# Half of an output projection as seven block products instead of eight, with operand sums and the residual formed by loads that add

## The chip, the core and the metric

The kernel runs on one core of a Trainium2 chip. The core has a matrix engine (TensorE, "PE" in the profile; its weight loads are "PEld"), a vector engine (VectorE, "DVE"), a scalar engine (ScalarE, "ACT"), GpSimd ("POOL") and SyncE ("SP"). All of them can issue DMA transfers, and 16 DMA engines carry these out between the chip's memory (HBM) and the on-chip memory SBUF. TensorE writes into PSUM banks, from which DVE or ACT must fetch the results ("evacuate" them). A load may also add what it reads to what stands in SBUF; in this kernel all such adding loads are issued by POOL. The metric is the device time of one execution in microseconds (us).

## What is computed

One transformer-like block over 512 tokens (rows) of width 2048, all in float32. Cut to what matters here:

```python
h = rmsnorm(x, norm_mix_pre)
proj = h @ w_in                                   # 512 x 5120
y_pool = pool_mixer(...proj...)                   # 512 x 1024
y_hgrn = hgrn2_mixer(...proj...)                  # 512 x 1024
mix = concatenate([y_pool, y_hgrn]) @ w_out       # 512 x 2048 @ 2048 x 2048
x = x + rmsnorm(mix, norm_mix_post)
h = rmsnorm(x, norm_mlp_pre)
ff = square(relu(h @ w_mlp_in)) @ w_mlp_out       # 2048 -> 8192 -> 2048
return x + rmsnorm(ff, norm_mlp_post)
```

`rmsnorm(x, w)` scales each row by one over its root mean square and each column by `w`.

## The kernel before

**Products in three matmuls.** Operands are split into a high part that the matrix engine takes exactly (`hi`) and the rest (`lo`); a product is hi x hi + hi x lo + lo x hi. So each raw tile is "split": ACT casts it to `hi`, DVE subtracts that from the raw tile to get `lo`. A weight tile has 4 x 128 rows and 512 columns (1 MB) and is split in two halves of 128x1024: two casts, two subtractions.

**Stages.** (1) The input projections `pj`, ten groups of four weight units, with the pooling mixer and the HGRN recurrence run beside them as small tasks. A `Clock` gives each task a step at every tick, that is after each block of matmuls. The mixers' results are stored as split pairs in `mixp`: `("h", c)` and `("p", c)` hold columns `c*512` to `c*512+511` of the two mixers, transposed, for all 512 tokens. (2) The output projection: four groups `om0` to `om3` of 512 columns each, in the function `gemm_group`. A group runs over the four pieces of the mixers' results (`MixActs`, rows of `w_out` in the order `mix_rows`) and in each over four row tiles of 128; 12 matmuls of 512 columns for each pair, 192 a group. The last group is merged: its last two weight units are taken together, so that a row tile is finished every second block. (3) The MLP, both halves, each as Strassen-Winograd products: 2x2 blocks, seven block products (`ORDER`) instead of eight, each in two "slots" (`q` = 0, 1). In the MLP's first half ("mi" in the profile) slots 0 to 15 treat 256 tokens by 512 columns; the second half ("al" and "ga") has 24 matmuls of 512 columns a slot. What DVE and ACT do beside a slot's matmuls is written out by hand in the table `plan`: for each slot a list to be issued ahead of the matmuls and one for their middle.

**Buffers and weights in the MLP.** Three raw buffers `X[0..2]` and two `YZ[0..1]` hold weights. `split_gen(k)` splits the weights of slot k during slot k-1 and then issues the next transfer into the same raw buffer: on POOL a load that adds the next block to it (the sums that Winograd's form wants), or on SP a plain load.

**From the projection to the MLP.** `evac_mix(n)` takes a finished 128x512 bank: ACT squares it for the norm's row sums (`ss_m`), DVE multiplies it by the post-norm's weights (`wpost`, loaded by POOL and scaled by ACT in `late_pools`, when the memory of stage 1 is given back) and writes it into `Y`. After group 3, `residual_task(t)` gets the row factor (`row_rstd`) and computes Y = Y * factor + x on DVE in four pieces of 512 columns, x having been loaded into SBUF (`load_xr`, POOL, four 1 MB loads ahead of group 2). Y is then the new x; it is stored by POOL (to `x2_dram` or straight to the output, for the residual at the end). `row_square` squares it on ACT for the second norm, in pieces of 128x512; when all are done `norm2_task` computes the row factors and spreads them over a tile (`row_bcast`, a 128x512 multiply by the identity on DVE and one matmul). `feed_in(tp, u, engine)` transposes Y (eight transposes into two banks, names `fps` in the profile) and evacuates them with the gain, on ACT or DVE, into the raw MLP operands `RM`. `split_in` splits these for the matmuls.

**Order.** Each engine executes its instructions in the order of the program, and so do the queues of SP and POOL: a transfer whose buffer is not free holds up all that were issued behind it on the same engine. The raw weight buffers turn over in time with the splits:

```python
more = {1: (1, 2), 5: (2, 2), 6: (2, 1), 3: (1, 2)}.get(i)
if more:
    nc.gpsimd.dma_start(raw, w_block(g, *more, q), accum_op=ALU.add)
elif i == 4:
    load_x(x + 3)
else:
    load_yz(n + 2)
```

## Time and profile before

| quantity | value |
|---|---|
| median of 3 runs | 1934.38 us (1933.76 to 1935.36) |
| the profiled execution, its time | 1934.39 us |
| span of that execution | 1932.4 us |
| granted TensorE clock, mean | 0.998 |
| TensorE busy | 1918.8 us (99%) |
| DVE busy | 1247.5 us (65%) |
| ACT busy | 836.3 us (43%) |
| POOL busy | 165.9 us (9%) |
| moved by DMA | 354.58 MB, 183 GB/s over the span |
| share of the 16 DMA engines: POOL's adding and other loads / SP's and others' | 40.2% / 27.3% |
| chain that ended last: matmuls of the output projection (`om`) | 9% of the span |
| MLP slot 0 begins at | 677.0 us |

The span runs from the first to the last recorded instruction on the chip; the execution's own time is 2.0 us longer. Line numbers (L266) are lines of the kernel. In the profile, `out<-in` are the names of tiles, `x24` is a count of instructions, and what stands in brackets is the idle time before an instruction and what ended it. "SPq" and "POOLq" are DMA issues; the last number of a DMA row is the median time in us from issue to landing. A row with `A:B` at its head is a stretch of the span: its length, then the busy time of PE, PEld, DVE, ACT and POOL with counts, the granted clock, the mean busy share of the DMA engines and GB/s. Matmuls overlap, so that the spacing of their starts and not the length of a record is what one takes.

### The profile page before, as it was taken

Reading aid. Unit: us, or ns where it says so; the run is one execution under the profiler, and the core shown is the slowest. Engines: PE = TensorE matmul, PEld = TensorE weight load, DVE = VectorE, ACT = ScalarE, POOL = GpSimd, SP = SyncE. Lnnn points to the kernel's source line nnn. Section 1 sums busy time; section 2 is a strip of 40 time slices with the busy share of each in tenths; the row PEclk is TensorE's granted clock in tenths of the full one; section 3 lists DMA queues with packets and bytes.
Section 4 is the critical chain, followed back from the end, with each engine's and each line's share of the span. In section 5 each row is a group of like instructions: output and inputs, shape, how many; then the busy total and the mean of one; then the engine's idle time right before and its main releaser. Section 6 shows DMA issues by size and latency. Waiting matters only on the chain.

```text
span 1932.4 us, 26089 instructions
## 1 busy us (share of the span) xinstructions
PE 1918.8 (99%) x10912; PEld 1634.9 (85%) x10912; DVE 1247.5 (65%) x1312; ACT 836.3 (43%) x996; POOL 165.9 (9%) x264
## 2 busy tenths in 40 slices
PE   9999999999999999999999999999999999999997
PEld 8888888888888899888888888888888888888886
DVE  5646344634623487576576665777777878878787
ACT  6321232123222376444444444446544444444455
POOL 3000000000000010101101101011010010010111
PEclk9999999999999999999999999999999999999999
DMA  8231222222252479988888889888898897897987
GB/s 316 88 109 67 88 88 88 89 88 98 83 200 88 174 196 240 203 233 217 204 228 201 217 217 217 261 220 235 214 245 220 199 237 228 208 230 209 234 212 149
DMA packets 56214, 354.58 MB, mean 183 GB/s; under 512 B 6048, under 2 KB 7072, under 8 KB 18592
## 3 DMA queue, kind: packets, MB, share of 16 engines
q0 software_dynamic: 25344, 163.06, 40.2%
q1 hardware_dynamic: 30608, 189.58, 27.3%
q8 instruction: 86, 1.41, 0.3%
q14 instruction: 32, 0.26, 0.0%
q10 hardware_dynamic: 144, 0.26, 0.0%
HBM read 327.72 MB, written 25.17 MB: 183 GB/s over the span
## 4 chain that ended last, share of the span: by engine, by line
PE 98%; DVE 1%; ACT 1%; issue 0%; DVEq 0%; POOL 0%; POOLq 0%; ACTq 0%
PE pj L266 23%; PE ps L1091 18%; PE al L1311 16%; PE ga L1311 12%; PE ps L1094 9%; PE om L266 9%; PE mi L1106 4%; PE la L1311 2%; PE lg L1311 2%; PE lps L633 1%; PE po L707 0%; PE fps L971 0%; PE po L709 0%; PE kvps L689 0%; PE warm_ps L403 0%; DVE ml L916 0%
## 5 line engine op out<-in xcount | busy, mean ns | idle before, releaser
L1091 PE MATMUL ps<-a,mh 128*128 128x512 f32 x1536 | 370.6, 391 | 0.0
L1091 PEld LDWEIGHTS ps<-a,mh 128*128 128x128 f32 x1536 | 280.9, 188 | 53.8 <-issue 0.3
L1311 PE MATMUL al<-mh,o 128*128 128x512 f32 x896 | 277.1, 389 | 0.0
L915 ACT CAST mh<-X 128x1024 fp32r<-128x1024 f32 x176 | 180.2, 1052 | 204.5 <-PE ps L1091 82.9
L915 ACT CAST mh<-YX 128x1024 fp32r<-128x1024 f32 x176 | 180.5, 1053 | 159.0 <-PE al L1311 46.3
L916 DVE TENSOR_TENSOR ml<-X,mh 128x1024 fp32r<-128x1024 f32 x176 | 207.3, 1219 | 54.4 <-ACT mh L915 54.2
L226 DVE TENSOR_TENSOR wl<-wr,wh 128x1024 fp32r<-128x1024 f32 (+1 forms) x118 | 136.1, 1169 | 157.2 <-ACT wh L225 157.1
L266 PE MATMUL pj<-xT,wh 128*128 128x512 f32 x760 | 235.7, 391 | 0.0
L916 DVE TENSOR_TENSOR ml<-YX,mh 128x1024 fp32r<-128x1024 f32 x176 | 207.3, 1220 | 31.0 <-ACT mh L915 30.9
L225 ACT CAST wh<-wr 128x1024 fp32r<-128x1024 f32 (+1 forms) x118 | 115.2, 1003 | 235.0 <-PE pj L266 153.6
L1311 PE MATMUL ga<-mh,o 128*128 128x512 f32 x672 | 208.0, 389 | 0.0
L1094 PEld LDWEIGHTS ps<-a,ml 128*128 128x128 f32 x1536 | 199.5, 191 | 9.0
L1094 PE MATMUL ps<-a,ml 128*128 128x256 f32 x1536 | 202.4, 283 | 0.0
L1311 PEld LDWEIGHTS al<-mh,o 128*128 128x128 f32 x896 | 168.2, 188 | 35.0
L1311 PE MATMUL al<-ml,o 128*128 128x512 f32 x448 | 174.3, 389 | 0.0
L266 PEld LDWEIGHTS pj<-xT,wh 128*128 128x128 f32 x760 | 141.5, 188 | 28.9
L266 PE MATMUL pj<-wh,xT 128*128 128x512 f32 x512 | 164.7, 395 | 0.0
L915 ACT CAST mh<-YZ 128x1024 fp32r<-128x1024 f32 x96 | 98.5, 1053 | 117.4 <-PE ps L1091 50.6
L1311 PEld LDWEIGHTS ga<-mh,o 128*128 128x128 f32 x672 | 126.1, 188 | 26.2
L266 PE MATMUL pj<-xT,wl 128*128 128x512 f32 x380 | 148.1, 390 | 0.0
L1140 DVE TENSOR_TENSOR t<-t,ps 128x512 f32<-128x512 f32 x120 | 82.4, 687 | 87.9 <-ACT t L1143 66.7
L916 DVE TENSOR_TENSOR ml<-YZ,mh 128x1024 fp32r<-128x1024 f32 x96 | 113.1, 1220 | 31.6 <-ACT mh L915 31.5
(249 smaller groups left out, 2635.7 us busy)
## 6 DMA issues: line engine op xcount, KB each, us to landing
wr<-in_w_in SPq DMA_DIRECT2D x38, 1024.0 KB, 4.9
X<-in_w_mlp_in POOLq DMA_DIRECT2D x33, 1024.0 KB, 9.1
X<-in_w_mlp_out POOLq DMA_DIRECT2D x33, 1024.0 KB, 8.3
YX<-in_w_mlp_in POOLq DMA_DIRECT2D x23, 1024.0 KB, 9.8
YX<-in_w_mlp_out POOLq DMA_DIRECT2D x23, 1024.0 KB, 9.2
YX<-in_w_mlp_in SPq DMA_DIRECT2D x21, 1024.0 KB, 5.7
YX<-in_w_mlp_out SPq DMA_DIRECT2D x21, 1024.0 KB, 5.0
wr<-in_w_out SPq DMA_DIRECT2D x16, 1024.0 KB, 4.9
```

What stands on the lines that cost most here:

```text
L225: nc.scalar.copy(out=hi[:, ks, :], in_=raw[:, ks, :])
L226: nc.vector.tensor_tensor(out=lo[:, ks, :], in0=raw[:, ks, :], in1=hi[:, ks, :].bitcast(F32), op=ALU.subtract)
L266: nc.tensor.matmul(bank, l, r, start=first and kt == 0 and oi == 0, stop=last and kt == 3 and oi == 2)
L633: nc.tensor.matmul(tiles[-1][r:r + mb, h % nh, w], K[:, h, w * P + r:w * P + r + mb], rhs[:, b0:b0 + nb, 1, :], start=True, stop=True)
L915: nc.scalar.copy(out=hi[:, ks, :], in_=raw[:, ks, :])
L916: nc.vector.tensor_tensor(out=lo[:, ks, :], in0=raw[:, ks, :], in1=hi[:, ks, :].bitcast(F32), op=ALU.subtract)
L1091: nc.tensor.matmul(o, hi[:, kt, ms], r, start=first and kt == 0, stop=q == 1 and kt == 3 and not first, skip_group_check=True)
L1094: nc.tensor.matmul(o[:, 0], lo[:, kt, ms], r[:, 0], start=False, stop=q == 1 and kt == 3, skip_group_check=True)
L1106: nc.tensor.matmul(o, l[:, kt, ms], r[:, x], start=st and oi == 0 and m % 2 == 0, stop=sp and oi == 2, skip_group_check=True)
L1140: nc.vector.tensor_tensor(out=t, in0=t, in1=half(banks, s_), op=sign)
L1311: nc.tensor.matmul(bank[h] if type(bank) is list else bank[:, h, :], a[:, l, kt, ts], r[:, kt, :], start=i in (1, 2, 5) and kt == 0 and oi ...
```

## The change

Columns 1024 to 2047 of the output projection (groups `om2` and `om3` before) become one product of 2x2 blocks: 256 tokens by 1024 inputs by 512 columns a block. A is the mixers' result (A11: tokens 0 to 255 and the pieces with c = 0; A12: the same tokens, c = 1; A21, A22: tokens 256 to 511) and B the weights. The seven products are P1 = A11 B11, P2 = A12 B21, P5 = (A21 - A22)(B11 + B12), P6 = (A21 - A22 - A11)(B11 + B12 + B22), P3 = (A21 - A22 - A11 + A12) B22, P7 = (A11 - A21)(B12 + B22) and P4 = A22 (B11 + B12 + B22 + B21), in this order, each in two slots of 24 matmuls of 512 columns: m = 0 to 13. The new parts are:

- `stash`: beside each of the 16 evacuations that write `mixp` in stage 1, ACT makes a signed raw copy (two activations of 128x256) and POOL stores it (256 KB) in `mix_dram`. `neg_hnw` holds a negated gain for it.
- `sums_task`, during `om1`, and `yx_room`: the operand sums are formed in raw tiles by a plain load on SP and adding loads on POOL, 512 KB each, and split (`split_sum`) on ACT and DVE.
- `mix_split_gen`: the weights of slot m + 1 are split ahead of slot m's matmuls, and the raw buffer then gets its next block by an adding load (POOL) or a plain load (SP). `X[0]`, `X[1]`, `YZ[0]` are loaded from `begin_mix`, `YZ[1]` from `yx_room` in slot 1. The last slots already issue loads and splits of the MLP's first slots.
- `products_mix` and `evac_half`: the matmuls, and the evacuation of each half with Winograd's sums, the squares and the weighing by `wpost`.
- `residual` and `rows_rstd`: Y is scaled in place by the row factor, a pair of row tiles at a time (on ACT, for tile 2 on DVE), and x is added to it by adding loads of POOL, 512 KB each. `load_xr` and `residual_task` are gone.
- `keep_x2`: the stores of the new x are issued by SP instead of POOL, for the first two row tiles in MLP slot 1, for the others in slot 4.
- `norm2_task`: one square of 128x2048 for each row tile, in place; the four follow one another at ticks of slots 4 to 7, and the row factors are computed behind the last.
- In `plan`, the second pair's residual is issued in slot 0, and one `feed_in` (1, 3) goes from ACT to DVE. Slot numbers in `plan` are the MLP's own, as before.

```diff
+    mix_dram = dram.tile([2, 2, 2, P, 4, 256], F32, name="mix_dram")
...
+    neg_hnw = const.tile([P, 8], F32, name="neg_hnw")
+    nc.gpsimd.tensor_scalar(out=neg_hnw, in0=vec[:, 32:40], scalar1=-1.0, scalar2=None, op0=ALU.mult)
...
-    for n in range(4):
+    for n in range(2):
...
+    def stash(c, q, k, src, scales):
+        sg = junk_tile([P, 512], "signed").rearrange("p (t s) -> p t s", t=2)
+        for t in range(2):
+            nc.scalar.activation(out=sg[:, t], in_=src[:, t * 256:(t + 1) * 256], func=AF.Copy,
+                                 scale=scales[(t + 1 + c) % 2])
+        nc.gpsimd.dma_start(mix_dram[c, q].rearrange("t p k s -> p t k s")[:, :, k, :], sg)
...
+                    stash(c, 1, j, y, (1.0, -1.0))
...
+                stash(c, 0, h, ps, (g, neg_hnw[:, 4 * c + h:4 * c + h + 1]))
...
+    def residual(t0, hs):
+        for h in hs:
+            for k in range(2):
+                t = t0 + k
+                yv = late["Y"][t][:, h * 1024:(h + 1) * 1024]
+                if t == 2:
+                    nc.vector.tensor_scalar(out=yv, in0=yv, scalar1=late["rt", t0][k], scalar2=None, op0=ALU.mult)
+                else:
+                    nc.scalar.activation(out=yv, in_=yv, func=AF.Copy, scale=late["rt", t0][k])
+                nc.gpsimd.dma_start(yv, x2d[t * P:(t + 1) * P, h * 1024:(h + 1) * 1024], accum_op=ALU.add)
...
+    def keep_x2(t):
...
-        rt = row_rstd(t)
-        for u in range(4):
-            us = slice(u * 512, (u + 1) * 512)
-            yv = Y[t][:, us]
-            nc.vector.scalar_tensor_tensor(out=yv, in0=yv, scalar=rt, in1=late["xr", t][:, us],
-                                           op0=ALU.mult, op1=ALU.add)
-            if t >= 2 and u == 1:
-                yield 1
         n_out = (D, D, D // 2, 0)[t]
         if n_out < D:
-            nc.gpsimd.dma_start(x2_dram[t * P:(t + 1) * P, 0:D - n_out], Y[t][:, 0:D - n_out])
+            nc.sync.dma_start(x2_dram[t * P:(t + 1) * P, 0:D - n_out], Y[t][:, 0:D - n_out])
         if n_out:
-            nc.gpsimd.dma_start(out2d[t * P:(t + 1) * P, D - n_out:D], Y[t][:, D - n_out:D])
-        if t < 1:
-            yield 3
-            row_square(t)
-    def row_square(t, us=range(4)):
-        for u in us:
-            junk = junk_tile([P, 512], "junk")
-            nc.scalar.activation(out=junk, in_=late["Y"][t][:, u * 512:(u + 1) * 512], func=AF.Square,
-                                 accum_out=ss2[:, t, u:u + 1])
+            nc.sync.dma_start(out2d[t * P:(t + 1) * P, D - n_out:D], Y[t][:, D - n_out:D])
...
     def norm2_task():
-        row_square(1)
-        yield 1
-        for t in (2, 3):
-            for h in range(2):
-                row_square(t, (2 * h, 2 * h + 1))
+        for t in range(NT):
+            yv = late["Y"][t]
+            nc.scalar.activation(out=yv, in_=yv, func=AF.Square, accum_out=ss2[:, t:t + 1])
+            if t < NT - 1:
                 yield 1
         ssr = small.tile([P, NT], F32, name="ssr")
-        nc.vector.tensor_reduce(out=ssr, in_=ss2, axis=AX.X, op=ALU.add)
-        mean_eps(ssr, ssr, D)
+        mean_eps(ssr, ss2, D)
...
-    def load_xr(i):
-        xr = pairs.tile([P, 2, D], F32, tag="pp", name=f"xr{i}")
-        for k in range(2):
-            t = 2 * i + k
-            nc.gpsimd.dma_start(xr[:, k], x2d[t * P:(t + 1) * P, :])
...
-            if n == 3:
-                clock.add(residual_task(t), (0, 0, 4, 3)[t])
...
+    def sums_task(q):
+        raw = late["tp2"].tile([P, 4, 256], F32, tag="tmp", bufs=4, name=f"sr{q}")
+        for i in (5, 6, 3):
+            SR[i, q] = raw
+        nc.sync.dma_start(raw, mix_dram[0, q, 1])
+        nc.gpsimd.dma_start(raw, mix_dram[1, q, 1], accum_op=ALU.add)
+        yield 5
+        split_sum(5, q)
+        nc.gpsimd.dma_start(raw, mix_dram[0, q, 0], accum_op=ALU.add)
+        yield 4
+        split_sum(6, q)
+        nc.gpsimd.dma_start(raw, mix_dram[1, q, 0], accum_op=ALU.add)
...
+    def mix_split_gen(m):
+        if m >= len(mslots):
+            yield from split_gen(m - len(mslots))
+            return
+        i, q = mslots[m]
+        raw, hi, lo = X[q] if i in (1, 5, 6, 4) else YZ[q], HI[m % 2], LO[m % 2]
+        for h in range(2):
+            ks = slice(2 * h, 2 * h + 2)
+            nc.scalar.copy(out=hi[:, ks, :], in_=raw[:, ks, :])
+            nc.vector.tensor_tensor(out=lo[:, ks, :], in0=raw[:, ks, :], in1=hi[:, ks, :].bitcast(F32),
+                                    op=ALU.subtract)
+            if h == 0:
+                yield
+        more = {1: (1, 2), 5: (2, 2), 6: (2, 1), 3: (1, 2)}.get(i)
+        if more:
+            nc.gpsimd.dma_start(raw, mix_block(*more, q), accum_op=ALU.add)
+        elif i == 2:
+            nc.sync.dma_start(raw, mix_block(2, 2, q))
+        elif i == 4:
+            load_x(q)
+        else:
+            load_yz(q)
...
+    def begin_mix(q):
+        X[q] = wraw.tile([P, 4, 512], F32, tag="raw", name=f"X{q}")
+        nc.sync.dma_start(X[q], mix_block(1, 1, q))
+        if q:
+            nc.sync.dma_start(YZ[0], mix_block(2, 1, 0))
...
+    for n in range(2):
+        if n == 1:
+            new_sum(5)
+            new_sum(6)
+            clock.add(sums_task(0), 1)
+            clock.add(sums_task(1), 2)
+        gemm_group(f"om{n}", MixActs(), False, evac_mix(n))
+    clock.drain()
...
+    def products_mix(m, hook):
+        i, q = mslots[m]
+        bank = oa if i in (1, 6, 7, 4) else og
+        hi, lo = HI[m % 2], LO[m % 2]
+        for h in range(2):
+            for kt in range(4):
+                if i in S:
+                    ah, al_ = (S[i][:, k, 4 * q + kt, h * P:(h + 1) * P] for k in range(2))
+                else:
+                    ts = slice((256 if i == 4 else 0) + h * P, (256 if i == 4 else 0) + (h + 1) * P)
+                    ah, al_ = (x[:, kt, ts] for x in mixp["hp"[q], 0 if i == 1 else 1])
+                for oi, (l, r) in enumerate(((ah, hi), (ah, lo), (al_, hi))):
+                    nc.tensor.matmul(bank[h], l, r[:, kt, :], start=i in (1, 2, 5) and q == 0 and kt == 0 and oi == 0,
+                                     stop=q == 1 and kt == 3 and oi == 2, skip_group_check=True)
+            hook(h)
...
+    def evac_half(m, h):
+        i, q = mslots[m]
+        if q == 0:
+            return
+        bank = (oa if i in (1, 6, 7, 4) else og)[h]
+        tp, n = {1: (1, 2), 2: (1, 2), 5: (2, 3), 3: (1, 3), 6: (1, 3), 7: (2, 3), 4: (2, 2)}[i]
+        t = 2 * tp - 2 + h
+        yv = late["Y"][t][:, n * 512:(n + 1) * 512]
+        if i in (1, 5, 3):
+            nc.scalar.copy(out=yv, in_=bank)
+            return
+        src = bank
+        if i != 4:
+            nc.vector.tensor_tensor(out=yv, in0=yv, in1=bank, op=ALU.add if i == 2 else ALU.subtract)
+            src = yv
+        junk = junk_tile([P, 512], "junk")
+        nc.scalar.activation(out=junk, in_=src, func=AF.Square, accum_out=ss_m[:, t, n:n + 1])
+        wp = late["wpost"][1][:, (n - 2) * 512:(n - 1) * 512]
+        def weigh():
+            nc.vector.tensor_tensor(out=yv, in0=src, in1=wp, op=ALU.mult)
+        if i == 4:
+            weigh()
+        else:
+            weighs.append(weigh)
...
+    def yx_room():
+        yx = pairs.tile([P, 2, 2048], F32, tag="pp", name="YX")
+        X[2], YZ[1] = (yx[:, h].rearrange("p (a b) -> p a b", a=4) for h in range(2))
+        RM[1, 1] = yx[:, 0].rearrange("p (a b) -> p a b", a=8)
+        nc.sync.dma_start(YZ[1], mix_block(2, 1, 1))
+        for q in range(2):
+            SR[7, q] = RM[1, 1][:, 4 * q:4 * q + 4]
+            nc.sync.dma_start(SR[7, q], mix_dram[0, q, 1])
+            nc.gpsimd.dma_start(SR[7, q], mix_dram[0, q, 0], accum_op=ALU.add)
...
+    mplan = {
+        1: ([yx_room], []),
+        2: ([lambda: new_sum(3), lambda: split_sum(3, 0)], []),
+        3: ([lambda: split_sum(3, 1)], []),
+        6: ([lambda: new_sum(7), lambda: split_sum(7, 0, True)], []),
+        7: ([lambda: split_sum(7, 1, True)], []),
+        8: ([ru_room], []),
+        10: ([lambda: residual(0, (0,))], []),
+        11: ([lambda: residual(0, (1,))], []),
+        12: ([lambda: new_act(1)], []),
+        13: ([], [lambda: feed_in(1, 0, "act"), lambda: split_first(0), lambda: split_first(1)]),
...
+        if m == 10:
+            weighs.pop(0)()
+            rstd_of(0)
+        run_weighs()
+        for _ in mix_split_gen(m + 1):
+            pass
+        for f in before:
+            f()
+        products_mix(m, mhook)
...
-        0: ([spl(1, 1, 1, 1)], [feed_step(1, 2, "act"), feed_step(1, 3, "act")]),
-        1: ([lambda: new_act(2), spl(2, 0, 1, 2)], []),
+        0: ([lambda: rstd_of(2), lambda: residual(2, (0,)), spl(1, 1, 1, 1)],
+            [feed_step(1, 2, "act"), lambda: residual(2, (1,)), feed_step(1, 3, "dve")]),
+        1: ([lambda: new_act(2), spl(2, 0, 1, 2), lambda: keep_x2(0), lambda: keep_x2(1)], []),
         2: ([spl(2, 1, 1, 2)], [feed_step(2, 0, "act")]),
         3: ([feed_step(2, 1, "act")],
             [feed_step(2, 2, "act"), s7(0), s7(1), lambda: clock.add(norm2_task(), 0)]),
-        4: ([feed_step(2, 3, "act"), new_pm, s1(0)], []),
+        4: ([feed_step(2, 3, "act"), new_pm, s1(0), lambda: keep_x2(2), lambda: keep_x2(3)], []),
```

More of the change, by code (lines that the diff above doesn't have):

```diff
@@ L1004, in hybrid_block, with new_sum, split_sum @@
-    behind["dma"] = [lambda: begin_x(0), lambda: begin_x(1)]
-    for n in range(4):
-        if n == 2:
-            load_xr(0)
-            load_xr(1)
-        last = n == 3
-        gemm_group(f"om{n}", MixActs(), False, evac_mix(n), merge=2 if last else 0,
-                   during=during_mix if last else None)
-    tp2, yp = late["tp2"], late["yp"]
+    S, SR = {}, {}
+    def new_sum(i):
+        S[i] = pairs.tile([P, 2, 8, 256], F32R, tag="pp", name=f"s{i}")
+    def split_sum(i, q, neg=False):
+        src = SR[i, q]
+        a = S[i][:, :, 4 * q:4 * q + 4]
+        nc.scalar.activation(out=a[:, 0], in_=src, func=AF.Copy, scale=-1.0 if neg else 1.0)
+        if neg:
+            nc.vector.scalar_tensor_tensor(out=a[:, 1], in0=src, scalar=-1.0, in1=a[:, 0].bitcast(F32),
+                                           op0=ALU.mult, op1=ALU.subtract)
+        else:
+            nc.vector.tensor_tensor(out=a[:, 1], in0=src, in1=a[:, 0].bitcast(F32), op=ALU.subtract)
@@ new lines, in hybrid_block, with mix_block @@
+    mslots = [(i, q) for i in ORDER for q in range(2)]
+    def mix_block(a, b, q):
+        return w_out[mix_rows[2 * a - 2 + q], 1 + b]
+    def mix_split_gen(m):
[20 more added lines that the diff above has]
+            load_yz(q)
@@ new lines, in ru_room, with rstd_of @@
+    def ru_room():
+        ru = pairs.tile([P, 2, 8, 256], F32, tag="pp", name="RU")
+        RM[2, 1], RM[1, 2] = ru[:, 0], ru[:, 1]
+    def rstd_of(t0):
+        late["rt", t0] = rows_rstd(t0)
+    mplan = {
[9 more added lines that the diff above has]
+        13: ([], [lambda: feed_in(1, 0, "act"), lambda: split_first(0), lambda: split_first(1)]),
+    }
@@ new lines, in split_first, with mhook @@
+    def split_first(k2):
+        ks = slice(2 * k2, 2 * k2 + 2)
+        src, a = raw_in(1, 1, 0)[:, ks], A[1][:, :, ks]
+        nc.scalar.copy(out=a[:, 0], in_=src)
+        nc.vector.tensor_tensor(out=a[:, 1], in0=src, in1=a[:, 0].bitcast(F32), op=ALU.subtract)
+    for m in range(len(mslots)):
+        before, amid = mplan.get(m, ([], []))
+        def mhook(h):
+            if m < 13:
+                evac_half(m, h)
+            if h == 0:
+                for f in amid:
+                    f()
+            elif m == 13:
+                feed_in(1, 1, "dve")
+            if m == 13:
+                evac_half(m, h)
+        if m == 10:
+            weighs.pop(0)()
+            rstd_of(0)
[3 more added lines that the diff above has]
+        for f in before:
+            f()
+        products_mix(m, mhook)
@@ L1021, in spl @@
+    tp2, yp = late["tp2"], late["yp"]
+    PA, PG = og, oa
     def spl(i, q, tp, kh, neg=False):
@@ L1357, in hybrid_block @@
     later = []
-    def rows_rstd(t0):
-        ss = small.tile([P, 2], F32, name="sst2")
-        m = small.tile([P, 2], F32, name="msq2")
-        y = small.tile([P, 2], F32, name="rt_y2")
-        r = small.tile([P, 2], F32, name="rt2")
-        nc.vector.tensor_reduce(out=ss, in_=ss_m[:, t0:t0 + 2, :], axis=AX.X, op=ALU.add)
-        nc.scalar.activation(out=y, in_=ss, func=AF.Sqrt, scale=1.0 / D, bias=eps_t)
-        mean_eps(m, ss, D)
-        nc.vector.reciprocal(out=y, in_=y)
-        nc.vector.tensor_tensor(out=r, in0=y, in1=y, op=ALU.mult)
-        nc.vector.tensor_tensor(out=r, in0=r, in1=m, op=ALU.mult)
-        nc.vector.scalar_tensor_tensor(out=r, in0=r, scalar=3.0, in1=y, op0=ALU.subtract, op1=ALU.mult)
-        return [r[:, k:k + 1] for k in range(2)]
     def add_scaled(t, c0, src, factor):
```

51 lines of the change are left out of this document (25 added, 26 removed).

## Prediction

> **What bounds the kernel now.** I read the page's engine table first, then the chain of waits, then busy time by stretch.
>
> ```profile
> span 1932.4 us, 26089 instructions
> PE 1918.8 (99%) x10912; PEld 1634.9 (85%) x10912; DVE 1247.5 (65%) x1312; ACT 836.3 (43%) x996; POOL 165.9 (9%) x264
> ...
> 528.33 141.45 PE om L266 x624
> ...
> 677.01 2.87 PE mi L1106 x24
> ...
> 700.78 0.88 PE fps L971 x8
> ...
> 588.00:677.00 89.00, 89.00 (x403) 73.92 (x402) 33.28 (x47) 27.26 (x49) 1.08 (x2) 1.00 0.38 139
> 677.00:776.00 99.00, 98.47 (x818) 97.41 (x817) 78.85 (x90) 70.17 (x111) 11.27 (x15) 1.00 0.81 214
> ...
> 1436.37:1490.77 54.40, 54.40 (x241) 45.05 (x240) 44.00 (x38) 25.87 (x25) 3.50 (x4) 1.00 0.80 224
> ```
>
> TensorE (PE) is never free. The chain of waits holds 624 out-projection matmuls in 141.45 us: one starts every 0.2267 us, although a record lasts 0.39. Columns 1024 to 2047 are the stretch from 588 to 677: there VectorE (DVE) is busy 33 of 89 us, ScalarE (ACT) 27, and the DMA engines 0.38 of the time (the column before the last). In the stretch behind it, MLP slots 0 to 15, DVE is busy 79 of 99 and DMA 0.81. So matmuls removed are worth their full spacing, if what replaces them finds room on DVE and DMA. The last row is the MLP's second half, which has the form of the new stage: 24 matmuls of 512 columns a slot, 54.40 us for ten slots, so 5.44 a slot with no wait.
>
> **The sum's reference.** The profiled execution took 1934.39 us, its span 1932.4 and 2.0 around it; the median of the three runs is 1934.38, the same.
>
> **Removed.** Eight block products become seven: 384 - 336 = 48 matmuls of 0.2267 us, **-10.9 us** (not 48 x 0.39). Transposes, row-sum matmuls and the MLP's matmuls stay in number. Sixteen DVE residual operations and the 4 MB load of x go as well; off the path they are worth nothing by themselves.
>
> **Signed copies and sums of the operands.** 32 ACT copies of 128x256 and sixteen 256 KB POOL stores go among the projections. ACT idles more than half the span (836 of 1932), POOL's queue is empty there and a weight split has a whole 10.9 us unit as its time: 0, and 0 to 1 if a copy waits for its buffer's store. The eight sum splits (one cast, one subtract each): four lie in group 1, at 1.0 and 1.1 us, beside units of 10.9; the other four go into slots 2, 3, 6, 7 and are counted below. The one POOL operation that negates a gain waits for a 36 KB load at the start, beside the masks: 0.
>
> **The last stored copy is late next.** The post-norm weights load on POOL only when the first stage's memory is free.
>
> ```profile
> 535.79 1.06 ACT L791 ACTIVATE wpost<-wpost 128x1024 f32<-128x1024 f32 x1 [5.95 <-DMA wpost<-in_norm_mix_post]
> ...
> 540.54 1.05 ACT L225 CAST wh<-wr 128x1024 fp32r<-128x1024 f32 x1
> ...
> 544.75 0.60 ACT L863 ACTIVATE junk<-om 128x512 f32<-128x512 f32 x1 [2.03 <-PE om L266]
> ...
> out<-YT ACTq DMA_DIRECT2D x1, 256.0 KB, 3.8
> ```
>
> If that includes the last store (3.8 us, the nearest row), ACT's multiplies and the casts behind them come some 3.5 us later. The second half of group 1's first split, with 1.2 of DVE, now ends at about 543, and group 1 starts at 544.7. 3.5 late, less that slack, less 1.4 because the half is needed only at the unit's seventh matmul: 0.4 (0 to 1.5).
>
> **Slots 2 to 4: weights too late.** Call the start of the 14 new slots T. Slot 1's work splits slot 2's weights; its second cast waits for slot 0's last matmul (T+5.7), and with 1.05 and 1.22 the split ends at T+8.0. Only then SP issues the reload of that buffer, and behind it, since SP goes in order, the first load of the other buffer, for slot 3.
>
> ```profile
> 646.09 0.33 SPq L900 DMA_DIRECT2D X<-in_w_mlp_in  x1
> 646.51 0.38 SPq L905 DMA_DIRECT2D YZ<-in_w_mlp_in  x1
> ...
> X<-in_w_mlp_in SPq DMA_DIRECT2D x1, 1024.0 KB, 4.8
> YZ<-in_w_mlp_in SPq DMA_DIRECT2D x1, 1024.0 KB, 6.9
> ...
> 1442.07 1.05 ACT L915 CAST mh<-YX 128x1024 fp32r<-128x1024 f32 x1 [1.68 <-PE al L1311]
> ...
> 1443.15 2.35 DVE L916 TENSOR_TENSOR ml<-YX,mh 128x1024 fp32r<-128x1024 f32 x2
> ...
> YZ<-in_w_mlp_in SPq DMA_DIRECT2D x1, 1024.0 KB, 6.8
> ```
>
> Two loads issued 0.42 apart landed after 4.8 and 6.9, so 2.5 us of the engines per MB. The last row is a load issued at 690.0 with an adding load in flight: 6.8 for 4.8. Slot 1's adding load is in flight here too, so the weights land at T+8.4+6.9 = T+15.3 to T+17.3. Slot 3 is due at T+16.3 and needs one cast and one subtract, 2.3: it waits 1.1 to 3.2; I take 3.0, as contention is sure. DVE then runs without a gap through two splits and two sum splits (6.8 us), and the evacuation behind them frees the bank that slot 4 starts: 1.1 more. Together **+4.1** (0 if the loads don't disturb each other, 5.5 at the most).
>
> **Slot 0 and 1 of the MLP.** Before, slot 0, with its sixteen transposes, took 7.33 us and slot 1, as most behind it, 5.76; DVE had 6.8 us of work in slot 0.
>
> ```profile
> 677.01:684.34 7.33, 7.33 (x65) 7.33 (x64) 6.78 (x12) 5.56 (x12) 1.78 (x2) 1.00 0.68 120
> 684.34:690.10 5.76, 5.76 (x51) 5.76 (x49) 3.96 (x5) 4.00 (x7) 0.56 (x1) 1.00 1.04 208
> ...
> 677.77 0.69 DVE L864 TENSOR_TENSOR Y<-om,wpost 128x512 f32<-128x512 f32 x1
> ...
> 682.12 0.15 DVE L799 TENSOR_REDUCE sst<-ss_m 128x1 f32<-128x4 f32 x1
> ...
> 683.08 0.16 DVE L804 SCALAR_TENSOR_TENSOR rt<-rt,rt_y 128x1 f32<-128x1 f32 x1
> ```
>
> Now DVE evacuates two pairs of transposes and weighs two tiles there (four of 0.69), has the row scale's chain (682.12 to 683.2), scales 128x1024 and splits an operand (1.2 each) and splits slot 1's weights (2.35): 2.8 + 1.1 + 2.4 + 2.35 = 8.7, so 1.4 late, and some 0.2 of waiting for ACT. The second half of the split is read only six of the slot's 48 matmuls later, 0.7: **+0.9** (0 to 1.5). Moving one evacuation from ACT to DVE is in it.
>
> **The adding loads of x.** The residual now comes by eight POOL loads of 512 KB that add, where x lay ready in SBUF. Adding loads queued behind each other:
>
> ```profile
> 1338.40 0.87 POOL L922 DMA_DIRECT2D YX<-in_w_mlp_out  x1 [3.67 <-DVE ml L916]
> 1343.30 0.87 POOL L922 DMA_DIRECT2D YZ<-in_w_mlp_out  x1 [4.04 <-DVE ml L916]
> 1348.74 0.87 POOL L922 DMA_DIRECT2D YX<-in_w_mlp_out  x1 [4.57 <-DVE ml L916]
> ...
> YX<-in_w_mlp_out POOLq DMA_DIRECT2D x1, 1024.0 KB, 12.1
> YZ<-in_w_mlp_out POOLq DMA_DIRECT2D x1, 1024.0 KB, 12.1
> YX<-in_w_mlp_out POOLq DMA_DIRECT2D x1, 1024.0 KB, 11.6
> ...
> X<-in_w_mlp_in POOLq DMA_DIRECT2D x1, 1024.0 KB, 8.0
> out<-YT POOLq DMA_DIRECT2D x5, 512.0 KB, 5.5
> ...
> out<-Y POOLq DMA_DIRECT2D x2, 1024.0 KB, 4.4
> ```
>
> They landed at 1350.5, 1355.4 and 1360.3: 4.9 us of all engines per MB, twice a plain load; alone 8.0 for 1 MB and 5.5 for half of one, so some 3 fixed. Call slot 0's start Z. On POOL's queue stand, in order: the weights added for slot 0, half of rows 256 to 511, the weights for slot 1, the other half: 4 MB, 19.6 us. SP's stores of rows 0 to 255 (2 MB at about 2, from 4.4 less the fixed part) and the next two weight loads (4.9) share the engines: 28.5. The first of POOL's four cannot issue before the weights are split (Z-2), moves data from Z+1, and rows 0 to 255 still have 1.5 to go. The other half lands at about Z+31.5. It is needed by the transposes in the middle of slot 3, at 700.78 where slot 0 began at 677.01: Z+23.8, with the wait above Z+24.7. PE stands in order, so it waits: **+7.0**. Ends: 0, if loads and stores of SP overlap with the adding ones at no cost, and 12, if halves cost more than half a MB does. I stand near the middle, by the row of 4.9, which is the same kind of transfer.
>
> The row of 6.8 says that SP's and POOL's transfers slow each other. The Trainium skill, "DMA: Bandwidth & Descriptors", section "Issuing engines are not separate DMA queues", has the rule: all issuing queues end on the same 16 engines; the trace agrees, and it speaks against this change. The same page, "Anatomy of one DMA", fits 2.0 us plus bytes at 436 GB/s, an estimated 4.4 us for 1 MB of any kind; the 8.0 above disagrees. By that figure the sum would lack these 7.0: 1931.3.
>
> **The second norm's tail.** Four squares of 128x2048 replace sixteen of 128x512, and the row scale follows slot 7 instead of slot 9.
>
> ```profile
> 727.77 2.35 DVE L916 TENSOR_TENSOR ml<-YZ,mh 128x1024 fp32r<-128x1024 f32 x2
> 730.04 1.22 DVE L951 TENSOR_TENSOR RU<-RU,A 128x1024 f32<-128x1024 f32 x1
> ...
> 740.15 0.16 DVE L844 TENSOR_REDUCE ssr<-ss 128x4 f32<-128x16 f32 x1
> ...
> 741.80 0.69 DVE L140 TENSOR_TENSOR rb_dg<-ident,rstd 128x512 f32<-128x512 f32 x1
> ...
> L1475 ACT ACTIVATE YX<-YX 128x2048 f32<-128x2048 f32 x1 | 1.9, 1912 | 0.0
> ...
> 728.26:735.06 6.80, 6.26 (x50) 5.86 (x49) 5.69 (x6) 5.67 (x11) 0.87 (x1) 1.00 0.85 152
> ```
>
> DVE is already late there: slot 8 (last row) takes 6.80 where its neighbours take 5.76, 1.0 of waiting. The norm's 2.3 us (740.15 to 742.4) and its wait for the last square (1.9, and the read behind it) now stand between slot 8's split and the operands of slot 9, where DVE has no room. Slot 9 then waits about 3.4 less the 1.0 there is: **+2.4** (-1.0 if lighter DVE work ahead takes up the lag, 4 if all of it shows).
>
> The stores of the new x move from POOL to SP. They stand ahead of weight loads that are due two slots later: 0; in the DMA sum they are counted.
>
> **Sum:** -10.9 + 0.4 + 4.1 + 0.9 + 7.0 + 2.4 = +3.9, so 1938.3 us.
>
> **Rivals.** (1) The rows of x land in time, the other waits stand: without the 7.0, 1931.3. For it: DMA is busy 0.81 in that stretch on average, not 1; against it, the sum above is 28.5 us of transfers for 23. (2) All waits are covered, as in the row of ten slots of 54.40 us, which has as many splits and adding loads a slot: -10.9 and the 0.4, so 1923.9. It decides from the point where slot 3's weights land before T+14.2; against it stands SP's order. (3) Halves of adding loads cost more than half: from 4.9 to 6.5 us per MB, 4 MB give 6.5 more, 1944.8.
>
> **Chances.** The forecast 0.50 (its own range 1934 to 1943; 0.33 of it slower by over 0.2%, 0.17 within), rival 1 0.25 (0.12 faster, 0.13 within), rival 2 0.15 (faster), rival 3 0.10 (slower). 0.2% is 3.9 us, about what a measurement of this kernel can tell from no change. So faster 0.27, within 0.30, slower 0.43. The range reaches from 1926, inside rival 2, to 1944, short of rival 3.
>
> **What the next profile would show.** 336 + 384 out-projection matmuls at 0.227. A PE wait of some 3 us before the fourth slot of the new stage, with ACT's cast released by a DMA, and one of 1 us at the fifth, released by DVE. In MLP slot 3 transposes that wait for a DMA into Y, with DMA share near 1 from slot 0. At slot 9 a wait for ACT and DVE. I am wrong if adding loads of 512 KB land within 8 us there, or if slot 3's weights land by T+14.

## The result, and the profile after

The changed kernel takes 1945.45 us (median of 6 runs, 1944.44 to 1950.59) against 1934.33 for the kernel before (1933.76 to 1935.36): a ratio of 1.0063, 95% interval 1.005 to 1.0076, so 11.1 us slower. The forecast was 1938.3, in a range of 1926 to 1944. The profiled execution took 1945.23.

The page's first lines and the longest pieces of the chain of waits in the part that differs:

```profile
span 1943.5 us, 26155 instructions
PE 1914.8 (99%) x10864; PEld 1629.0 (84%) x10864; DVE 1264.4 (65%) x1316; ACT 872.4 (45%) x1029; POOL 190.4 (10%) x296
...
530.91 3.11 DMA mix_dram<-signed
535.58 7.32 DMA wpost<-in_norm_mix_post
...
599.02 9.11 DMA YX<-in_w_out
610.56 28.57 PE og L1089 x119
...
659.42 9.65 DMA X<-in_w_mlp_in
...
685.16 22.15 DMA Y<-in_x
```

There are 48 matmuls fewer, as meant. But where the chain had TensorE alone, five transfers now stand in it: the store of the last signed copy and the post-norm weights behind it, the weights for slot 3 (`YX` here is the tile that holds `YZ[1]`), the weights for MLP slot 0, whose sum heads POOL's queue, and the last adding load of x, 22 us long.

Busy time by stretch, the kernel before: groups 0 and 1, groups 2 and 3, MLP slots 0 and 1, slots 2 and 3, slots 4 to 7, slots 8 to 11. The first number behind the bounds is the length.

```profile
495.35:588.01 92.66, 92.66 (x409) 76.58 (x408) 44.82 (x46) 27.69 (x39) 3.38 (x6) 1.00 0.40 143
588.01:676.85 88.84, 88.84 (x402) 73.77 (x401) 33.13 (x47) 27.26 (x49) 1.08 (x2) 1.00 0.38 139
676.85:690.10 13.25, 13.25 (x114) 13.25 (x112) 10.90 (x16) 9.56 (x17) 2.35 (x3) 1.00 0.83 156
690.10:705.16 15.06, 15.06 (x131) 14.89 (x129) 13.21 (x19) 10.75 (x21) 1.09 (x2) 1.00 0.88 312
705.16:728.26 23.10, 23.10 (x195) 23.10 (x194) 19.66 (x19) 19.79 (x34) 1.80 (x2) 1.00 0.60 142
728.26:753.18 24.92, 24.39 (x196) 23.49 (x195) 20.50 (x25) 17.20 (x26) 3.47 (x4) 1.00 0.97 186
```

The changed kernel, the same stretches in the same order (the last one ends at slot 12, 764.29); then within the 14 new slots: slot 1, slot 2, slot 3, slots 4 to 12.

```profile
495.35:590.62 95.27, 93.54 (x409) 76.43 (x408) 49.05 (x50) 34.13 (x51) 9.96 (x13) 1.00 0.56 159
590.62:673.33 82.71, 79.76 (x354) 65.49 (x352) 47.37 (x52) 46.62 (x63) 11.47 (x14) 0.98 0.95 233
673.33:688.62 15.29, 14.17 (x115) 13.57 (x114) 13.60 (x22) 11.68 (x19) 4.73 (x6) 1.00 1.04 285
688.62:714.10 25.48, 17.94 (x131) 17.24 (x129) 9.71 (x10) 10.40 (x19) 0.00 (x0) 0.80 1.02 295
714.10:737.21 23.11, 23.11 (x196) 23.11 (x193) 19.46 (x18) 19.98 (x24) 1.70 (x2) 1.00 0.59 132
737.21:764.29 27.08, 25.34 (x197) 23.61 (x195) 20.00 (x24) 17.36 (x21) 3.95 (x5) 1.00 0.83 161
596.06:601.50 5.44, 5.44 (x25) 4.50 (x24) 2.38 (x2) 1.65 (x2) 0.00 (x0) 1.00 0.91 164
601.50:609.30 7.80, 5.60 (x25) 4.32 (x23) 0.02 (x1) 1.68 (x3) 0.00 (x0) 1.00 0.99 391
609.30:617.21 7.91, 7.15 (x25) 5.59 (x25) 7.48 (x7) 5.10 (x6) 2.55 (x3) 0.78 0.82 181
617.21:666.17 48.96, 48.96 (x218) 40.54 (x216) 31.82 (x37) 30.38 (x41) 7.63 (x9) 1.00 0.97 221
```

Subtract the two tables: groups 0 and 1 +2.6, the new stage -6.1, slots 0 and 1 +2.0, slots 2 and 3 +10.4, slots 4 to 7 nothing, slots 8 to 11 +2.2: together +11.1, all of it. Nine of the new slots take 48.96, exactly 9 x 5.44; slots 2 and 3 take 4.8 too much, which is what is missing of the 10.9.

Two columns to look at: the DMA share (last but one) is 0.95 to 1.04 from the new stage to MLP slot 3, where the old projection had 0.38 and the old slots 0 to 3 had 0.83 and 0.88; and the clock (the one before) is 0.98 and 0.80 where TensorE waited. The matmuls behind a long wait run slower:

```profile
606.72:609.30 2.58, 0.38 (x2) 0.00 (x0) 0.02 (x1) 1.09 (x2) 0.00 (x0) 1.00 1.01 414
609.30:613.30 4.00, 3.24 (x8) 2.35 (x9) 4.00 (x4) 4.00 (x5) 1.70 (x2) 0.58 0.61 129
699.49:704.37 4.88, 0.28 (x4) 0.10 (x2) 2.47 (x3) 1.99 (x2) 0.00 (x0) 0.77 1.05 306
704.37:707.35 2.98, 0.45 (x1) 0.15 (x1) 2.76 (x3) 0.00 (x0) 0.00 (x0) 0.50 1.02 232
707.35:710.35 3.00, 3.00 (x14) 3.00 (x15) 0.00 (x0) 1.68 (x4) 0.00 (x0) 0.50 0.89 283
710.35:714.10 3.75, 3.75 (x28) 3.75 (x26) 0.60 (x1) 0.16 (x1) 0.00 (x0) 0.73 1.04 431
```

In slot 3 of the MLP 7.6 of the 10.0 us lost are waiting (4.9 and 3.0, less the usual time of two matmuls); the rest is work at a clock of 0.50 and 0.73 behind it (3.00 x 0.50 + 3.75 x 0.27 = 2.5).

The queues show why the loads are late. SP issues the load for slot 3 behind the reload of the other buffer; POOL issues x's second half behind the weight sums:

```profile
598.60 0.33 SPq L1044 DMA_DIRECT2D YZ<-in_w_out  x1
599.02 0.62 SPq L1130 DMA_DIRECT2D YX<-in_w_out  x1
...
672.88 0.85 POOL L933 DMA_DIRECT2D X<-in_w_mlp_in  x1 [11.70 <-DVE ml L927]
679.10 1.73 POOL L848 DMA_DIRECT2D Y<-in_x  x2 [5.37 <-DVE Y L845]
683.96 0.85 POOL L933 DMA_DIRECT2D X<-in_w_mlp_in  x1 [3.13 <-DVE ml L927]
684.63 1.94 POOL L848 DMA_DIRECT2D Y<-in_x  x2
```

### The profile page after: what moved, and what is told of

Read it like the earlier page. It is cut to its first block, busy times and chain, and to the rows that moved or that the text cites. A ratio compares the mean times of both kernels' runs of the same rounds, so it can differ in the third digit from the quotient of the medians.

```text
span 1943.5 us, 26155 instructions
## 1 busy us (share of the span) xinstructions
PE 1914.8 (99%) x10864; PEld 1629.0 (84%) x10864; DVE 1264.4 (65%) x1316; ACT 872.4 (45%) x1029; POOL 190.4 (10%) x296
## 2 busy tenths in 40 slices
DMA packets 60662, 371.35 MB, mean 191 GB/s; under 512 B 6656, under 2 KB 7680, under 8 KB 22784
## 4 chain that ended last, share of the span: by engine, by line
PE 83%; issue 8%; DMA 4%; DVE 2%; ACT 2%; POOL 1%; SPq 0%; DVEq 0%; POOLq 0%; ACTq 0%
PE ps L1261 18%; PE al L1481 16%; PE pj L269 15%; PE ga L1481 12%; PE ps L1264 9%; PE la L1481 2%; PE om L269 2%; PE og L1276 2%; PE lg L1481 2%; PE og L1089 1%; DMA Y<-in_x 1%; PE oa L1276 1%; PE oa L1089 1%; DMA xt<-in_x_t 1%; PE lps L645 1%
## 5 line engine op out<-in xcount | busy, mean ns | idle before, releaser
L926 ACT CAST mh<-X 128x1024 fp32r<-128x1024 f32 x176 | 180.2, 1053 | 209.7 <-PE ps L1261 82.9
L229 DVE TENSOR_TENSOR wl<-wr,wh 128x1024 fp32r<-128x1024 f32 (+1 forms) x100 | 117.0, 1181 | 130.9 <-ACT wh L228 130.9
L228 ACT CAST wh<-wr 128x1024 fp32r<-128x1024 f32 (+1 forms) x100 | 98.9, 1013 | 191.0 <-PE pj L269 153.2
L269 PEld LDWEIGHTS pj<-xT,wh 128*128 128x128 f32 x760 | 141.5, 188 | 28.9
```

The source lines that it names most:

```text
L228: nc.scalar.copy(out=hi[:, ks, :], in_=raw[:, ks, :])
L229: nc.vector.tensor_tensor(out=lo[:, ks, :], in0=raw[:, ks, :], in1=hi[:, ks, :].bitcast(F32), op=ALU.subtract)
L269: nc.tensor.matmul(bank, l, r, start=first and kt == 0 and oi == 0, stop=last and kt == 3 and oi == 2)
L926: nc.scalar.copy(out=hi[:, ks, :], in_=raw[:, ks, :])
```

## The experiments

The question was which of the losses belong to the change and which to the order of issue around it. Theory A: each wait has its own place in a queue and goes when that is altered. Theory B: the change moves 371.35 MB where it was 354.58, most of the surplus into one stretch, and any order only moves the wait. Stage lengths in the table are from the profiled executions, the times are medians of 4 to 11 runs; all kernels compute the full result.

| kernel | median us | ratio to before, 95% | groups 0, 1 | 14 slots | slots 0, 1 | 2, 3 | 4 to 7 | 8 to 11 |
|---|---|---|---|---|---|---|---|---|
| before | 1934.3 | | 92.7 | (88.8) | 13.3 | 15.1 | 23.1 | 24.9 |
| changed | 1945.45 | 1.005 to 1.0076 | 95.3 | 82.7 | 15.3 | 25.5 | 23.1 | 27.1 |
| x first | 1939.51 | 1.0018 to 1.0038 | 95.4 | 83.0 | 15.3 | 16.9 | 26.0 | 27.1 |
| YZ[1] first | 1942.22 | 1.0027 to 1.006 | 93.7 | 80.1 | 15.1 | 25.9 | 23.1 | 28.2 |
| pools by tile | 1942.39 | 1.0028 to 1.0057 | 92.7 | 83.2 | 15.3 | 25.4 | 23.1 | 27.1 |
| norm's tail later | 1942.26 | 1.0027 to 1.0057 | 94.2 | 83.9 | 15.3 | 24.6 | 23.1 | 24.5 |
| x first, sums last | 1935.45 | 0.9995 to 1.0014 | 94.9 | 82.9 | 15.3 | 14.9 | 23.1 | 28.6 |
| YZ[1] first, DVE lighter | 1942.99 | 1.0028 to 1.0056 | 95.1 | 79.1 | 14.9 | 24.5 | 23.1 | 27.1 |
| scaling behind the split | 1948.31 | 1.0058 to 1.0085 | 95.3 | 82.8 | 13.8 | 28.6 | 23.1 | 28.6 |
| all | 1927.99 | 0.9954 to 0.9979 | 92.7 | 79.2 | 13.5 | 18.1 | 23.1 | 24.5 |
| all, sums later still | 1931.76 | 0.9978 to 0.9996 | 92.7 | 79.3 | 13.5 | 18.1 | 27.0 | 25.1 |
| all, scaling first again | 1925.84 | 0.9944 to 0.9969 | 92.7 | 78.8 | 15.2 | 14.9 | 23.1 | 24.5 |

Groups 0 and 1 differ between the profiled executions of kernels in which nothing about them was altered (93.7 to 95.4, against 92.7 with no wait), and so do slots 8 to 11 (27.1 or 28.2 to 28.6, see the end). A single edit is therefore judged by its own column.

**x first.** The loads that add to the weights of slots 0 and 1 are held until x's loads stand in the queue.

```diff
         if more:
-            nc.gpsimd.dma_start(raw, w_block(g, *more, q), accum_op=ALU.add)
+            def add():
+                nc.gpsimd.dma_start(raw, w_block(g, *more, q), accum_op=ALU.add)
+            if k < 2:
+                held.append(add)
+            else:
+                add()
...
-            [feed_step(1, 2, "act"), lambda: residual(2, (1,)), feed_step(1, 3, "dve")]),
+            [feed_step(1, 2, "act"), lambda: residual(2, (1,)), release, feed_step(1, 3, "dve")]),
```

> The changed kernel with one order altered: the adding loads that turn the raw weights of MLP slots 0 and 1 into the sums for slots 6 and 7 (1 MB each, POOL) are issued behind the second pair's four adding loads of x instead of ahead of them. Theory A (order): TensorE waits in slot 3 because the last half of x stands behind 2 MB that nobody needs before slot 5. Without them the engines have from 676.4 on 2 MB of adding loads (9.8 us by 4.9 a MB) and 2 MB of stores (4), so x lands near 691 to 695, the transposes due at 699.5 do not wait, slot 3 falls from 17.4 to 7.5 us and the time to about 1935 (1934 to 1937). The weight sums then land near 705, ahead of their split at 708. Theory B (volume): the 16 engines have 28 to 31 us of work for 26 us in any order; then the wait moves to slots 5 and 6, where the sums are read, and the time stays within 3 us of 1945.4.

The last half of x was issued at 686.1 and landed at 695.9 (it had needed 22.15 us), and the transposes no longer waited for it. Slots 2 and 3 lost 8.6 of their 10.4, but slots 4 to 7 grew by 2.9: 1939.51, where A had said at most 1937. POOL's queue and the chain of waits of this kernel:

```profile
685.55 1.72 POOL L848 DMA_DIRECT2D Y<-in_x  x2 [3.81 <-DVE Y L845]
686.63 2.40 POOL L940 DMA_DIRECT2D X<-in_w_mlp_in  x2
...
694.84 16.19 DMA YX<-in_w_mlp_in
```

The sums are issued in the same breath as x, and the plain loads for slots 4 and 5, issued on SP at 689.9 and 694.8, now took 13.6 and 16.2 us. So A holds for x; what remains could be order again, or B.

**x first, sums last.** To tell these apart, the two sums wait, by a one-column copy on POOL that reads slot 3's split weights, until 694.2 and 694.9.

```diff
+        nc.gpsimd.tensor_copy(gates[:, n:n + 1], LO[k % 2][:, 3, 0:1].bitcast(F32))
+        held.pop(0)()
...
         w_split_all(k + 1)
+        if k == 2:
+            release_behind(3)
+            release_behind(3)
```

> As the kernel with x first, but the two held adding loads of weight sums now wait (by a one-column copy on POOL) until slot 3's weights are split, near 695, so that they no longer run ahead of the plain loads for slots 4 and 5. In the kernel with x first those loads took 13.6 and 16.2 us from issue to landing and slots 3 and 5 were still 1.9 and 1.5 longer than before. Theory A (order): with the plain loads ahead they land in 5 to 8 us, slots 3 and 5 lose these 3.4 us, the sums land near 706 to 709 in time, and the time is about 1936. Theory B (volume): the same bytes must pass before slot 6, so the wait goes to slots 5 and 6 and the time stays at 1938 to 1940.

Busy time of slots 2 and 3 and of slots 4 to 7 in this kernel:

```profile
688.39:703.28 14.89, 14.89 (x130) 14.89 (x129) 8.61 (x9) 10.11 (x19) 2.03 (x4) 1.00 1.01 254
703.28:726.39 23.11, 23.11 (x195) 23.11 (x194) 20.46 (x19) 20.00 (x24) 1.70 (x2) 1.00 1.02 297
```

No wait is left in these six slots, although the DMA engines' share is 1.01 and 1.02. (The plain loads for slots 4 and 5 took 8.6 and 9.2 us, not the 5 to 8 that A had said, and were in time even so.) That was order, not volume: 10 us of the whole time, in a kernel that differs from the changed one by when two loads are issued.

**YZ[1] first.** In slot 1 the load of `YZ[1]` is issued ahead of the split that ends with the reload of `YZ[0]`; the loads for S7 stay behind it, in a function `s7_loads`.

```diff
...
+        if m == 1:
+            yx_room()
         for _ in mix_split_gen(m + 1):
             pass
```

> The changed kernel with SP's order altered in new slot 1: the first load of YZ[1], for slot 3, is issued ahead of the reload of YZ[0] (for slot 6) instead of behind it; the operand loads of S7 stay behind. Theory A: slot 3's wait of 4.8 us (2.5 of waiting for the load, the rest for ACT, DVE and at the lower granted clock) is only SP's order. The load can be issued when slot 0 has ended (596.1 instead of 599.0) and without a load ahead of it lands near 603 to 605; slots 2 and 3 take 5.44 each and the time falls to about 1940.6 (1939.5 to 1942). Theory B (volume): the load still shares the engines with the adding loads and lands at 606 or later; half of the wait stays, 1943.

New slots 2 and 3 take 12.74 together, where 10.88 is free of waits and the changed kernel had 15.71. The load was issued 5.6 us after the stage's start instead of 8.4 and landed 14.8 after it instead of 17.5; it still took 9.2 us beside the adding load for slot 5, the reload and S7's loads. Some 0.8 of waiting for the load is left in slot 3, and what had stood behind that wait came out: 1.1 at slot 4's start for a bank that DVE had not yet emptied. A for the larger part, B for the 9.2; the time, 1942.22, lies between the two theories (at most 1942, and 1943).

**YZ[1] first, DVE lighter.** In addition S7's plain loads go to slot 3 and the splits of S3 to slots 4 and 5 (the cut is against the changed kernel).

```diff
...
-        1: ([yx_room], []),
-        2: ([lambda: new_sum(3), lambda: split_sum(3, 0)], []),
-        3: ([lambda: split_sum(3, 1)], []),
+        3: ([s7_loads], []),
+        4: ([lambda: new_sum(3), lambda: split_sum(3, 0)], []),
+        5: ([lambda: split_sum(3, 1)], []),
```

> As the kernel with YZ[1] first, and besides the two plain loads for S7 (1 MB, SP) move from new slot 1 to slot 3 and the split of the sum S3 from slots 2 and 3 to slots 4 and 5. With YZ[1] first its load still took 9.2 us beside three others, slot 2 waited 1.1 for it and slot 3 1.3 more for a bank behind four splits on DVE. Theory A: without the S7 loads YZ[1] lands in 7 to 8 us, DVE has two splits fewer at that place, slots 2 and 3 take 5.44 to 5.7 each, and all 14 slots with their transposes take 78.0 to 78.3 us against 82.7; the time is 1939.5 to 1940.5. Theory B: the bound is the adding loads for slots 4 and 5 that run there anyway; slots 2 and 3 keep over 1 us of waiting.

Slots 2 and 3 now take 11.77: the wait for the bank went with DVE's two splits, 0.9 for the load stays. The load took 9.2 us again, where A had said 7 to 8: S7's loads beside it were not what made it slow. The 14 slots missed the 78.3 by 0.8. The whole time did not follow (1942.99 in the median, over runs of 1939.7 to 1944.5, of which the profiled one is the fastest); its other stages still had their waits.

**Pools by tile.** The memory pools `yp` and `tp2` are opened with `reuse_waits="tile"`, so that a tile waits for the tiles whose memory it takes and not for everything in the first stage's.

> The changed kernel with the late memory pools waiting for the tiles that they overlap only, and not for everything in the first stage's memory. Theory A: the post-norm weights land 5.4 us later than before because their load waits for the last signed copy's store (landed 534.0). If that store's buffer is not under them, they are issued at about 531.6 and land some 3.5 us sooner; group 1's start loses 2.4 of its 2.6 us: 1943.0. Theory B: the load itself is slower because the sums' first 512 KB load runs beside it (6.5 and 7.3 us from issue to landing); then at most 1 us comes back, 1944.5. If the buffers overlap, nothing changes.

The wait is gone, 92.67 as before. POOL's queue in the changed kernel, and then in this one:

```profile
530.91 0.72 POOL L462 DMA_DIRECT2D mix_dram<-signed  x1 [3.48 <-ACT signed L460]
535.02 1.11 POOL L803 DMA_DIRECT2D wpost<-in_norm_mix_post  x2 [3.38 <-DMA mix_dram<-signed]
```

```profile
530.33 0.72 POOL L462 DMA_DIRECT2D mix_dram<-signed  x1 [3.48 <-DVE mp L548]
531.05 1.11 POOL L803 DMA_DIRECT2D wpost<-in_norm_mix_post  x2
```

The first names its releaser, the last copy's store; the second has none. B's slower load is there too (6.0 and 6.7 us here, 4.4 and 5.4 in the kernel before), but costs nothing by itself.

**Norm's tail later.** `yield 2` behind the last square.

> The changed kernel with the second norm's row factors computed two ticks later, behind slot 9's weight split, as before the change, and not behind slot 7. Theory A: the 2.3 us of small DVE operations and their wait for the last square, ahead of slot 9's operands, are what make slots 8 and 9 longer by 3.0 us together (of which 1.7 are given back later); slots 8 to 11 come back to 25.8 us or less and the time falls by 2.2 to 1943.2. Theory B: DVE is late there with or without the tail (it was 1.0 late in the kernel before, with the tail in slot 9), and the time stays within 0.7 of 1945.4.

Slots 8 to 11 take 24.50, 2.6 less than in the changed kernel and 0.4 less than before the change. A.

**Scaling behind the split.** `residual(2, (0,))` goes from the list ahead of slot 0's matmuls to the one in their middle.

> The changed kernel with the first scaling of rows 256 to 511 (one on ACT, one on DVE) issued in MLP slot 0 behind the split of slot 1's weights instead of ahead of it. Theory A: slots 0 and 1 are 2.0 us longer than before because ACT and DVE have this scaling in front of slot 1's split; they lose 1.2 to 1.8 of it. The adding loads of x start 1.5 to 2 us later, and the wait in slot 3 grows by as much: the sum stays the same, 1944 to 1946. Theory B: DVE's work is too long in any order (8.7 us and more for 7.5); slots 0 and 1 stay within 0.4 of 15.3.

Slots 0 and 1 lost 1.5, as A said, but slots 2 and 3 grew by 3.1 and the time is 1948.31, for at most 1946. POOL's queue, and the waits of TensorE behind it (in total, how often, the longest):

```profile
682.11 1.16 POOL L933 DMA_DIRECT2D X<-in_w_mlp_in  x1 [8.27 <-DVE ml L927]
682.77 4.00 POOL L848 DMA_DIRECT2D Y<-in_x  x4
...
PE fps L982 <- DMA Y<-in_x: 11.5, 2, 7.3
```

The split of slot 1's weights now ends first, so that both weight sums stand ahead of all of x. The last load of x landed where it did before, 34.0 us behind slot 0's start; but the first two landed 24.2 and 28.9 behind it, for 16.3 and 18.8. TensorE waited for them in slot 2, 7.3 and 4.2 us, where it had waited 7.1 in slot 3. A's wait that only grows in slot 3 is not what happened.

**All.** The edits above together.

> All reorderings together: pools waiting by tile, YZ[1] first, S7's loads and S3's splits later, scaling behind the split in slot 0, x ahead of the weight sums and these behind slot 3's split, the norm's tail two ticks later. No operation is left out. Theory A (each wait is one of order): group 1 starts without its wait, 14 slots in 78.2, slots 0 to 3 in 28.8, slots 4 to 11 in 48: that is the 10.9 us of the 48 matmuls less about 1 of small waits, 1924 to 1926, 0.45% below the kernel before. Theory B (volume: 17 MB more are moved than before, and the second projection half is followed at once by the densest stretch): at least a third of the 22 us comes back as other waits, 1930 or more.

1927.99 is 6.3 below the kernel before, between the two theories: A for groups 0 and 1 and slots 8 to 11, and for the new stage but for 1.0 us (79.2 for 78.2); but slots 2 and 3 kept 3.0 us. Its x loads (2 MB) were issued at 676.6 to 678.2 and landed at 682.1, 685.0, 689.6 and 694.6; the transposes in the middle of slots 2 and 3 waited for the second and the last. Two ways out were tried.

**All, sums later still.** The gate reads slot 4's split (`if k == 3: release_behind(4)`, twice).

> As the kernel with all reorderings, but the two held adding loads wait for slot 4's split instead of slot 3's. In that kernel they were issued at 686.8, while the last half of x was in flight (issued 678.2, landed 694.6), and slots 2 and 3 still took 8.55 and 9.54 us for 7.57 and 7.49 before. Theory A (order): without them x lands at about 690, slot 3 takes 7.5 to 8, slot 2 stays near 8.5 since its half had landed before; the sums land by 706, when slot 5 splits the first: the time is 1926.0 to 1926.8. Theory B: the engines have too little room left, and the sums come late for slots 6 and 7: no gain, 1927.5 or more.

A is refuted: x landed at 694.57 again, since the sums had stood behind it in any case. Its last two halves landed 4.2 and 5.0 us apart, beside the plain loads that SP had issued at 681.9 and 686.3; in the kernel with x first, halves with hardly another load beside them landed 2.6 and 2.7 apart. So these plain loads are the likely cause, though no run moved them alone. And the sums, now issued at 696.8 and 698.0, landed at 710.3 and 717.6, too late for slots 6 and 7: slots 4 to 7 took 27.0. So B has a share: the stretch has no room for a transfer that is moved back by 10 us.

**All, scaling first again.** `plan` for slot 0 as in the changed kernel, the rest as in "all".

> As the kernel with all reorderings, but with the scaling of rows 256 to 511 ahead of the weight split in slot 0, as in the changed kernel. x's loads start some 2.5 us earlier in the slot and slot 1's split 1.5 us later. Theory A: slot 1 waits 1.5 (7.25 for 5.76), slots 2 and 3 have no wait (7.4 and 7.5): slots 0 to 3 take 30.2 us against 31.6, and the time is about 1926.6. Theory B: what is gained at x is lost elsewhere behind it, 1928.

1925.84, ratio 0.9956 (0.9944 to 0.9969): 8.4 us faster than the kernel before, the best version. Slots 0 to 3 take 30.05 us. Of the 10.9 us it gets 10.1 in the new stage (88.84 to 78.78), less 1.9 in slots 0 and 1, and 0.4 back in slots 8 to 11. The profiled execution, 1924.86, is the fastest of its five: its groups began at 494.5, 0.8 us earlier than in the kernel before, where the profiles of all these kernels range from 494.5 to 495.9.

## Why the prediction was wrong

The places were right: but for slot 4's bank, every wait that the prediction named was there, with the releaser that it named, and the change was slower. The sum was +3.9 and should have been +11.1. The step that failed is the price of a long wait: the sum takes a wait of TensorE at its length and gives nothing for the matmuls behind it, which ran at half the clock, 3.9 of the 7.2 us that are missing. Beside it two terms left their own ranges: group 1's start (2.2 too little) and MLP slots 0 and 1 (1.1 too little). The rest (without the clock, 0.9 more for x, 0.7 less for slots 2 to 4, 0.2 less for the norm's tail) is size within the ranges.

| step | predicted | measured |
|---|---|---|
| 48 matmuls of 0.2267 | -10.9 | -10.9 (48.96 for nine slots) |
| group 1's start | +0.4 (0 to 1.5) | +2.6 in the profiled execution |
| new slots 2 to 4 | +4.1 (0 to 5.5) | +4.8 |
| MLP slots 0 and 1 | +0.9 (0 to 1.5) | +2.0 |
| adding loads of x | +7.0 (0 to 12) | +10.4 |
| second norm's tail | +2.4 (-1.0 to 4) | +2.2 |

- **Group 1's start.** The store's part was right (issued at 535.02 for 531.31). Missed was the rest: the post-norm weights themselves took 6.5 and 7.3 us, for 4.4 and 5.4; SP's 512 KB load for the sums, issued at 534.17, and the adding load on it, issued at 537.72, ran beside them. So they landed 5.4 to 5.9 later and not 3.5. The prediction gave these loads no price; that they are what slowed the weights was not tested apart.
- **New slots 2 to 4.** The load landed at 608.13, T+17.5, just behind the interval of T+15.3 to T+17.3. Bound and cause were right. The wait for the bank (1.1) did not add up with it, since while TensorE waits DVE catches up; it came to light when the first wait was gone. In its place stood the slow clock. (The prediction's own interval gives a wait of 1.3 to 3.3, where it writes 1.1 to 3.2.)
- **Slots 0 and 1.** The list of DVE's work was complete for slot 0, but it began late, behind two splits of operand halves (0.69 each) that the last new slot issues; and DVE then waited 1.4 for ACT's cast, which stood behind a scaling of 1.15. The prediction had taken 0.2 for that wait, from the 0.24 of the kernel before. In the other direction, the scaling takes DVE 0.75 and not 1.2.
- **The adding loads.** The prediction said Z+31.5, though its terms add up to Z+31.0 (1.0 + 1.5 + 28.5), which is a wait of 6.3 and not 7.0; they landed at 707.31, Z+34.0. Rows 0 to 255 had landed at Z+3.1 and not Z+2.5, and the 28.5 us of transfers took 30.9. The need was at 699.5 and not at Z+24.7 (698.0), because of the waits ahead: 7.6 to 7.8 of waiting for 7.0. The price for a MB was nearly right: in the kernel with x first, four halves landed at 685.8, 688.4, 691.1 and 695.9, 2.6 and 2.7 us apart where hardly anything else ran with them, so 5.3 a MB for 4.9; rival 3 (halves dearer than half, 6.5 a MB) falls, although its 1944.8 is near the result. Some 2.5 of the 3.4 us missing here are the low clock.
- **The clock** is the term that was left out altogether: about 1.4 in new slot 3 (8 matmuls in 3.24 us for 1.8) and 2.5 in MLP slot 3, 3.9 of the 7.2 us. In the kernel before TensorE was never idle for more than 0.4 us in these stages and the clock stayed at 1.00, so none of its rows showed the price. The Trainium skill, "TensorE: Matmul & The Clock Gate", "Part 1: The HAM clock gate", states half the clock after an idle window of about 3.4 us, and the full one after as long of activity; the trace agrees with its half (0.50 in the row from 704.37), and here idle times of 2.2 and 0.8 us with one matmul between them were enough. A price for a wait of 3 us should have had that added.
- **Rivals.** The first (x in time) needed two loads in another order; with that it was 1935.45, not 1931.3, since the other waits were larger than that sum allowed. The second (all waits covered, 1923.9) is nearly the best version, 1925.84; its condition, that slot 3's weights land before T+14.2, is just missed there (T+14.7), and 0.8 of that wait remains.

## What to carry to other kernels

When work is taken off a bound engine, list what each queue must issue in the stage that follows, with the deadline of every transfer: here the 10.9 us were real, and 10 of the 22 us of new waits came from two adding loads that were issued over 40 us before anyone read their result. Put transfers in the queue by when they are needed, not by when their buffer comes free; but a saturated stretch forgives neither direction, as a delay of 10 us cost 4. Here two waits in one place (slot 3's weights, slot 4's bank) did not add up, and the long waits cost more than their length.
